# The last gate block's working tiles moved into idle buffers, its two halves interleaved, and three output weight loads given other tiles

## The chip, the cores and the metric

The kernel runs on one core of one Trainium2 chip. The metric is the device time of one execution in microseconds (us). Each version is run several times and the median is compared; a trace of one profiled execution shows where the time goes. All times below are from the start of that execution's span.

## The reference

One decoder block over 1024 positions and width 1024, in float32. What matters here, cut from the reference:

```python
h = rmsnorm(x, norm_g[l]) * (1.0 + scale) + shift
q, k, v, g_attn, xr, g_rnn, m_attn, m_rnn = split(h @ w_in[l])
y_attn = sliding_window_attention_with_sinks(q, k, v, sinks) * silu(g_attn)
xr = causal_depthwise_conv(xr, conv_w, conv_b)               # width 4
# RG-LRU: per block of 256 channels
r = sigmoid(xr @ wa + ba);  i = sigmoid(xr @ wx + bx)
a = exp(-LRU_C * r * softplus(-lam));  b = sqrt(1 - a*a) * (i * xr)
hs[t] = a[t] * hs[t-1] + b[t]                                # scan over time
y_rnn = hs * silu(g_rnn)
merged = sigmoid(m_attn) * (y_attn @ w_attn_proj) + sigmoid(m_rnn) * (y_rnn @ w_rnn_proj)
x = x + gate * (merged @ w_out);  return rmsnorm(x, final_g)
```

## The kernel before

**Products in three terms.** Every float32 operand of TensorE is split into a high part (a cast by ScalarE, `wh`, `nh`, `hh`, `mh`) and the remainder (a subtraction by VectorE, `wl`, `nl`, `hl`, `ml`); a product is high·high + low·high + high·low. `cast` (L101) makes `wh`, `rest` (L107) makes `wl`; both have five buffers.

**The projection stage.** Pairs of column blocks of `w_in` go through a seven-product scheme (`Pair`, L533 forms the weight sums `ws`, L571 joins two results). One product is 12 matmuls of 128x512 (L511) and fills one *slot*; a pair takes seven slots, k = 0 to 6, whose moving operands are named hha, nh, nh, nh, hh, hh, nh in this order. In slot 1 TensorE needs the low part of S1, in slot 5 that of S4, in slot 6 that of S3, in slot 0 that of A11: always from the second matmul of the slot on, for which VectorE must have run L107. Loads of raw weights are `r<-w_main`. L614 is the tanh of a result `c`, and `smr_d<-c` stores it.

**The recurrent branch** runs inside this stage in four blocks `hb`, each of two halves `oc`, so eight chunks c = 2·hb + oc of 128 channels. The convolution leaves `xch` (tag `xa`, two buffers) and `xcl` (tag `xcl`, two buffers). `extra` puts the gate product (24 matmuls, L794, tile `pgate`) of a half between two slots. `after_gates` then lists the ten pieces that follow for a half:

- ScalarE: Sigmoid to `rz` (a1, L809) and to `it` (a2, L812), Tanh to `th` (a3, L824), Exp to `av` and Square (a4, a5, L827, L830), Sqrt (a6, L837), the cast `yh` (a7, L852).
- VectorE: `rz` scaled (d1, L815), `it`·conv (d2, L819), `th` (d3, L833), `it` (d4, L840), the scan (d5, L845), `rz`·`gg` (d6, L849), the remainder `yl` (d7, L856).

`gg` is the silu gate, read back from DRAM (`sgr_d`); its tile shares a buffer with `th` (tag `th`, one buffer), and its load is issued at the end of d4. `yl` shares the buffer `it`, and `yh` the buffer `av`. `start_gates` queues these pieces, with gaps of a slot; `background` puts a piece on its engine when its planned time fits. Each engine then works its own list in this fixed order.

**Opening of attention.** After the last piece of c = 7 the pool of the recurrent branch (tags rz, it, th, av, xc, xcl, xa) is closed and the attention pool is opened over it: `sink`, `ks`, `qs` are loaded by SP, and the first score product (`s_ps`, L1033) follows in TensorE's list. One pair of the projection stage and the RNN projection (`rp`) are interleaved with attention.

**The tail.** `merged` is made per chunk (`tt`, L1487 to L1501). `load_wo(k)` loads a chunk of `w_out` into `wo32` (tag `tt`, two buffers, shared with the merge), multiplies it by the gate row (L1454), casts it (L1457) and subtracts (L1458); the last product (L1522) runs over eight row tiles, the first three of them together, by chunk k. Here a list scheduler sets the order. `tail` is a pool with the tags `xo` (x reloaded), `o` (three buffers for results) and `fst`.

SP issues nearly all DMAs, one queue in order; it waits for the release of a buffer before it issues the load into it, and what is behind waits too.

Of the kernel before, what the change touches and what calls it, by code (L numbers as in the profile page):

```python
# [12 lines left out]
F32 = mybir.dt.float32  # L13
# [9 lines left out]
P = 128  # L23
S = 1024
D = 1024
KC = 8
# [25 lines left out]
def tile_hybrid_block(ctx, tc, x, pk, rows, posr, posi, invf, c_row, w_ss, w_gate, w_main, w_v,  # L52
# [4 lines left out]
    def dma(dst, src, eng=nc.sync):  # L57
        dst, src = (a.bitcast(F32) if a.dtype == F32R else a for a in (dst, src))
        return eng.dma_start(dst, src)  # L59
# [75 lines left out]
    sgr_d = [tc.dram_tile([P, S], F32, name=f"sgr_d{c}") for c in range(KC)]  # L135
# [5 lines left out]
    hb = ctx.enter_context(tc.tile_pool(name="hb", bufs=1))  # L141
# [37 lines left out]
    with ExitStack() as st:  # L179
# [102 lines left out]
        tt = tiny("tt")  # L282
# [114 lines left out]
    W = {}  # L397
# [69 lines left out]
    waiting = [], []  # L467
# [15 lines left out]
    def slots(d):  # L483

        t = []

        def f():
            t.append(W["slot"])
            return W["slot"] >= t[0] + d
        return f  # L490
# [258 lines left out]
    def ask(hb, oc):  # L749

        if ("g", (hb, oc)) not in W and (hb, oc) not in gq:
            gq.append((hb, oc))
        return ("g", (hb, oc)) in W

    def second(hb):

        gq.append((hb, 1))
        W["free", hb, 1] = Load.act + 0.4
        return True

    def start_gates(hb):

        load1, split1 = gate_weights(hb, 1)
        c0, c1 = after_gates(hb, 0), after_gates(hb, 1)
        waiting[0].append(lambda: ask(hb, 0))
        one, two = [], [lambda: ask(hb, 1)]
        for todo, steps_ in ((one, c0), (two, c1)):
            for i, step in enumerate(steps_):
                gap = hb < 3 or i in ((0, 3, 5) if todo is one else (0, 3, 5, 7))
                todo.extend(step + ([slots(1)] if gap else []))  # L770
                if todo is one and i == 1:
                    todo.append(lambda: second(hb))
        if hb == 3:
            one.insert(0, lambda: W.setdefault("rush", True))
        waiting[0].extend(one + two)
        waiting[1].extend([load1, slots(2)] + split1)
        return True

    def extra():

        if not gq or Load.pe < max(W.get((n_, *gq[0]), d_) for n_, d_ in (
                ("ready", 1e9), ("free", 0.0))):
            return 0.0
        hb, oc = gq.pop(0)
        wh, wl = W["gw", hb, oc]
        res = []
        for which in range(2):
            ps = psm.tile([P, 1024], F32, tag="main", name="pgate")
            for ic in range(2):
                h_, l_ = W["xc", hb, ic][:2]  # L790
                c0 = which * 256 + ic * P
                for i, (ww, xx_) in enumerate(((wh, h_), (wl, h_), (wh, l_))):
                    for hf in range(2):
                        W["pe"] = T.matmul(ps[:, SL[hf]], ww[:, c0:c0 + P], xx_[:, SL[hf]],  # L794
                                           start=(ic == 0 and i == 0),
                                           stop=(ic == 1 and i == 2))
            res.append(ps)
        W["g", (hb, oc)] = res
        return GATE

    def after_gates(hb, oc):
        c, t = 2 * hb + oc, {}

        def tl(n, tag=None, dt=F32):
            t[n] = W["rn"].tile([P, S], dt, tag=tag or n, name=n)
            return t[n][:]

        def a1():
            A.activation(tl("rz"), W["g", (hb, oc)][0][:], AF.Sigmoid, bias=pcol(PK_BA, c))  # L809

        def a2():
            A.activation(tl("it"), W["g", (hb, oc)][1][:], AF.Sigmoid, bias=pcol(PK_BX, c))  # L812

        def d1():
            V.scalar_tensor_tensor(out=t["rz"][:], in0=t["rz"][:], scalar=pcol(PK_BSH, c),  # L815
                                   in1=rbig[:], op0=ALU.mult, op1=ALU.max)

        def d2():
            V.tensor_tensor(out=t["it"][:], in0=t["it"][:], in1=W["xc", hb, oc][2][:],  # L819
                            op=ALU.mult)  # L820
            W["used", c] = True

        def a3():
            A.activation(tl("th"), t["rz"][:], AF.Tanh)  # L824

        def a4():
            A.activation(tl("av"), t["rz"][:], AF.Exp, scale=-1.0)  # L827

        def a5():
            A.activation(t["rz"][:], t["av"][:], AF.Square)  # L830

        def d3():
            V.scalar_tensor_tensor(out=t["th"][:], in0=t["rz"][:], scalar=1.0, in1=t["th"][:],  # L833
                                   op0=ALU.add, op1=ALU.mult)

        def a6():
            A.activation(t["th"][:], t["th"][:], AF.Sqrt, scale=2.0 ** 20)  # L837

        def d4():
            V.scalar_tensor_tensor(out=t["it"][:], in0=t["th"][:], scalar=2.0 ** -10,  # L840
                                   in1=t["it"][:], op0=ALU.mult, op1=ALU.mult)
            dma(tl("gg", "th"), sgr_d[c])

        def d5():
            V.tensor_tensor_scan(out=t["rz"][:], data0=t["av"][:], data1=t["it"][:],  # L845
                                 initial=0.0, op0=ALU.mult, op1=ALU.add)

        def d6():
            V.tensor_tensor(out=t["rz"][:], in0=t["rz"][:], in1=t["gg"][:], op=ALU.mult)  # L849

        def a7():
            A.copy(tl("yh", "av", F32R), t["rz"][:])  # L852
            dma(yh_d[c], t["yh"][:], G if c == KC - 1 else nc.sync)

        def d7():
            V.tensor_tensor(out=tl("yl", "it", F32R), in0=t["rz"][:], in1=f32(t["yh"][:]),  # L856
                            op=ALU.subtract)
            dma(yl_d[c], t["yl"][:], G if c == KC - 1 else nc.sync)

        return [[[("A", 2.4, 0, a1)]], [[("A", 1.11, 0, a2), ("D", 0, 1.28, d1)]],  # L860
                [[("A", 2.35, 0, a3)], [("D", 0, 1.22, d2)]],
                [[("A", 1.06, 0, a4), ("A", 1.06, 0, a5)]], [[("D", 0, 1.22, d3)]],
                [[("A", 2.35, 0, a6)]], [[("D", 0, 1.22, d4)], [("D", 0, 2.29, d5)]],
                [[("D", 0, 1.22, d6)]], [[("A", 1.05, 0, a7)]], [[("D", 0, 1.22, d7)]]]

# [506 lines left out]
    late, high, loaded = [], [], {}  # L1372
# [76 lines left out]
    wo = [None] * KC  # L1449

    def load_wo(k, pool, tag):
        w32 = tpool.tile([P, D], F32, tag="tt", name="wo32", bufs=2)
        dma(w32[:], w_out[k * P:(k + 1) * P, :])
        V.tensor_tensor(out=w32[:], in0=w32[:], in1=gate_bc[:], op=ALU.mult)  # L1454
        t = pool.tile([P, 2, D], F32R, tag=tag, name="wo")
        h_, l_ = t[:, 0, :], t[:, 1, :]
        A.copy(h_, w32[:])  # L1457
        V.tensor_tensor(out=l_, in0=w32[:], in1=f32(h_), op=ALU.subtract)  # L1458
        wo[k] = (h_, l_)
# [197 lines left out]
```

## Time and profile before

| what | value |
|---|---|
| median of 3 runs | 937.59 us (937.12 to 939.36) |
| the profiled execution, its own time | 937.05 us |
| its span, first to last instruction | 935.3 us |
| TensorE matmuls busy | 908.0 us of the span (97%) |
| VectorE busy | 688.0 us (74%) |
| ScalarE busy | 533.7 us (57%) |
| GpSimd busy | 109.0 us (12%) |
| mean granted TensorE clock | 0.996 |

In the profile's rows the first number is the start, the second the duration, both in us; "x12" is a count of instructions merged into a row; brackets at the end give the idle time of the engine before the row and what ended it. PE is TensorE, ACT is ScalarE, DVE is VectorE, POOL is GpSimd, SPq is the DMA queue of SP. In a table of windows the columns behind the stretch are its length, the busy time of each engine with the number of its instructions, the granted clock of TensorE, the busy share of the DMA engines, and GB/s.

### The profile page before, as it was taken

Reading aid. Unit: us, or ns where it says so; the run is one execution under the profiler, and the core shown is the slowest. Engines: PE = TensorE matmul, PEld = TensorE weight load, DVE = VectorE, ACT = ScalarE, POOL = GpSimd, SP = SyncE. Lnnn points to the kernel's source line nnn. Section 1 sums busy time; section 2 is a strip of 40 time slices with the busy share of each in tenths; the row PEclk is TensorE's granted clock in tenths of the full one; section 3 lists DMA queues with packets and bytes.
Section 4 is the critical chain, followed back from the end, with each engine's and each line's share of the span. In section 5 each row is a group of like instructions: output and inputs, shape, how many; then the busy total and the mean of one; then the engine's idle time right before and its main releaser. Section 6 shows DMA issues by size and latency. Waiting matters only on the chain.

```text
span 935.3 us, 12434 instructions
## 1 busy us (share of the span) xinstructions
PE 908.0 (97%) x4261; PEld 752.4 (80%) x4261; DVE 688.0 (74%) x1068; ACT 533.7 (57%) x1040; POOL 109.0 (12%) x161
## 2 busy tenths in 40 slices
PE   5899999999999999999999988999999999999997
PEld 3689888878888888888887877888888888888786
DVE  8978888777669965996676675899999737656522
ACT  7435565454567656775696584888888622212311
POOL 1046000000000000000000001354454300000000
PEclk9999999999999999999999999999999999999999
DMA  8923587951332541354145348997655186436311
GB/s 313 374 68 125 167 283 231 310 191 46 113 112 91 187 151 50 136 175 136 57 157 170 101 138 280 320 333 238 218 177 188 57 315 224 159 125 234 132 72 67
DMA packets 81141, 164.20 MB, mean 176 GB/s; under 512 B 12772, under 2 KB 29156, under 8 KB 81079
## 3 DMA queue, kind: packets, MB, share of 16 engines
q1 hardware_dynamic: 77734, 155.32, 49.0%
q0 software_dynamic: 2192, 6.00, 1.9%
q10 hardware_dynamic: 1152, 2.10, 0.6%
q8 instruction: 33, 0.54, 0.2%
q14 instruction: 30, 0.24, 0.1%
HBM read 114.00 MB, written 49.78 MB: 175 GB/s over the span
## 4 chain that ended last, share of the span: by engine, by line
PE 75%; DVE 10%; DMA 6%; ACT 5%; issue 4%; SPq 0%; POOL 0%; ACTq 0%; DVEq 0%
PE bk L511 41%; PE rp L169 9%; PE pmain L169 4%; PE pgate L794 4%; PE rp L1522 3%; PE pmain L1522 3%; PE s_ps L1033 3%; PE pv L1105 2%; DMA wo<-w_out 2%; DMA tt<-tr_d 1%; PE pt L1071 1%; DVE wl L107 1%; PE bk L169 1%; DMA smr<-smr_d 1%; DVE wo L1458 1%
## 5 line engine op out<-in xcount | busy, mean ns | idle before, releaser
L511 PE MATMUL bk<-nh,wl 128*128 128x512 f32 x368 | 144.4, 392 | 3.7 <-DVE wl L107 3.7
L511 PE MATMUL bk<-nl,wh 128*128 128x512 f32 x368 | 143.9, 391 | 0.0
L511 PE MATMUL bk<-nh,wh 128*128 128x512 f32 x368 | 143.9, 391 | 0.0
L107 DVE TENSOR_TENSOR wl<-r,wh 128x512 fp32r<-128x512 f32 x108 | 79.0, 735 | 18.3 <-ACT wh L101 18.3
L511 PEld LDWEIGHTS bk<-nh,wl 128*128 128x128 f32 x368 | 69.4, 189 | 19.9 <-DVE wl L107 5.5
L101 ACT CAST wh<-r 128x512 fp32r<-128x512 f32 x108 | 66.4, 618 | 32.4 <-DMA r<-w_ap 12.3
L511 PEld LDWEIGHTS bk<-nh,wh 128*128 128x128 f32 x368 | 69.5, 189 | 14.4
L511 PEld LDWEIGHTS bk<-nl,wh 128*128 128x128 f32 x368 | 69.5, 189 | 14.3
L511 PE MATMUL bk<-hh,wl 128*128 128x512 f32 x184 | 71.8, 390 | 1.7 <-DVE wl L107 1.7
L511 PE MATMUL bk<-hh,wh 128*128 128x512 f32 x184 | 71.6, 389 | 0.0
L511 PE MATMUL bk<-hl,wh 128*128 128x512 f32 x184 | 71.6, 389 | 0.0
L59 POOL DMA_DIRECT2D yh_d<-yh x1 | 0.6, 583 | 479.2 <-ACT yh L852 479.2
L107 DVE TENSOR_TENSOR wl<-ws,wh 128x512 fp32r<-128x512 f32 x80 | 54.2, 681 | 1.9 <-ACT wh L101 1.9
L1057 ACT ACTIVATE p<-p,small 128x129 f32<-128x129 f32 x128 | 50.1, 400 | 0.0
L101 ACT CAST wh<-ws 128x512 fp32r<-128x512 f32 x80 | 48.0, 615 | 2.2 <-DVE ws L533 1.2
L511 PEld LDWEIGHTS bk<-hh,wl 128*128 128x128 f32 x184 | 34.6, 188 | 9.6 <-DVE wl L107 2.6
L511 PEld LDWEIGHTS bk<-hh,wh 128*128 128x128 f32 x184 | 34.6, 188 | 7.2
L511 PEld LDWEIGHTS bk<-hl,wh 128*128 128x128 f32 x184 | 34.5, 188 | 7.1
L1033 PE MATMUL s_ps<-ks,qs 128*128 128x256 f32 (+1 forms) x256 | 37.6, 289 | 0.1
L1539 ACT ACTIVATE o<-xo 128x1024 f32<-128x1024 f32 (+2 forms) x10 | 8.9, 889 | 47.5 <-DVE xo L1538 47.5
L511 PE MATMUL bk<-hha,wh 128*128 128x512 f32 x92 | 35.9, 391 | 0.0
L511 PE MATMUL bk<-hha,wl 128*128 128x512 f32 x92 | 35.8, 389 | 0.0
(356 smaller groups left out, 2255.6 us busy)
## 6 DMA issues: line engine op xcount, KB each, us to landing
r<-w_main SPq DMA_DIRECT2D x100, 256.0 KB, 4.1
wada<-w_ss SPq DMA_DIRECT2D x16, 512.0 KB, 8.4
qs<-q_d SPq DMA_DIRECT2D x16, 512.0 KB, 5.4
ks<-k_d SPq DMA_DIRECT2D x24, 192.0 KB, 3.8
xt<-x SPq DMA_DIRECT2D x8, 512.0 KB, 6.3
q_d<-rhi SPq DMA_DIRECT2D x16, 256.0 KB, 3.9
q_d<-rlo SPq DMA_DIRECT2D x16, 256.0 KB, 2.9
wg<-w_gate SPq DMA_DIRECT2D x8, 512.0 KB, 4.6
```

Source lines behind the costliest of these rows:

```text
L101: A.copy(dst[0][:], src)
L107: V.tensor_tensor(out=dst[1][:], in0=src, in1=f32(dst[0][:]), op=ALU.subtract)
L169: mm = T.matmul(ps[hf], ww, xx[kc][hf], start=(kc == 0 and ww is w_h and xx is xh), stop=(kc == KC - 1 and xx is xl))
L511: W["pe"] = T.matmul(ps, ww[:, c], b[kc][xx_], start=(first and kc == 0 and i == 0), stop=(kc == 3 and i == 2), skip_group_check=not first)
L794: W["pe"] = T.matmul(ps[:, SL[hf]], ww[:, c0:c0 + P], xx_[:, SL[hf]], start=(ic == 0 and i == 0), stop=(ic == 1 and i == 2))
L1033: W["pe"] = T.matmul(o, qs[:, j, qc], ks[:, b, k0 + (0 if n else P):k0 + 256], start=(b == 0), stop=(b == 1))
L1057: A.activation(px[:, j, :], px[:, j, :], AF.Exp, bias=sm[:, 0, j:j + 1], accum_out=sm[:, 1, j:j + 1])
L1071: W["pe"] = T.transpose(pt[:, j, :], px[:, j, 0:P], ident[:])
L1105: W["pe"] = T.matmul(pv[:], b, m[:].rearrange("p j q -> p (j q)"), start=(i == 0), stop=(i == len(prods) - 1))
L1458: V.tensor_tensor(out=l_, in0=w32[:], in1=f32(h_), op=ALU.subtract)
L1522: T.matmul(ps[:, sl], lhs[k][th][:, ts_], w[:, sl], start=(k == 0 and w is h_ and lhs is mh), stop=(k == KC - 1 and lhs is ml))
L1539: A.activation(o[:, sl], xo[:, sl], AF.Square, accum_out=fs[:, i:i + 1])
```

## The change

Four edits, three of them for the last block (hb = 3, c = 6 and 7):

1. The `gg` of c = 6 and c = 7 get tiles of the tag `xcl` (dead once the gate product of c = 7 has read it) and are both loaded directly behind that product, instead of at the end of their d4.
2. `rz` and `it` of c = 7 get tiles of the tag `xa` (dead at the same time) in place of the buffers of c = 6.
3. `start_gates` lists the pieces of the two halves interleaved: the Sigmoid a1 of c = 7 goes before the last pieces of c = 6.
4. The `wo32` of k = 4, 5 and 6 use the tag `o` of the pool `tail` in place of `tt`.

```diff
@@ start_gates
-        one, two = [], [lambda: ask(hb, 1)]
-        for todo, steps_ in ((one, c0), (two, c1)):
...
+        if hb < 3:
...
+        else:
+            gap = [None]
+            for item in ([[lambda: W.setdefault("rush", True)], c0[0], gap, c0[1],
+                          [lambda: second(hb)], c0[2], c0[3], gap, c0[4], c0[5], gap, c0[6],
+                          [lambda: ask(hb, 1)], c1[0], c0[7], gap, c0[8], c1[1], c0[9], c1[2],
+                          c1[3], gap, c1[4], c1[5], gap, c1[6], c1[7], gap, c1[8], c1[9]]):
+                waiting[0].extend([slots(1)] if item is gap else item)
@@ extra
         W["g", (hb, oc)] = res
+        if (hb, oc) == (3, 1):
+            for c in (KC - 2, KC - 1):
+                W["gg", c] = W["rn"].tile([P, S], F32, tag="xcl", name="gg", bufs=2)
+                dma(W["gg", c][:], sgr_d[c])
@@ after_gates
         def tl(n, tag=None, dt=F32):
-            t[n] = W["rn"].tile([P, S], dt, tag=tag or n, name=n)
+            late = c == KC - 1 and n in ("rz", "it")
+            t[n] = W["rn"].tile([P, S], dt, tag="xa" if late else tag or n, name=n,
+                                bufs=2 if late else 1)
@@ d4
-            dma(tl("gg", "th"), sgr_d[c])
+            if hb < 3:
+                dma(tl("gg", "th"), sgr_d[c])
+            else:
+                t["gg"] = W["gg", c]
@@ load_wo
-        w32 = tpool.tile([P, D], F32, tag="tt", name="wo32", bufs=2)
+        w32 = (tail.tile([P, D], F32, tag="o", name="wo32", bufs=3) if 4 <= k < 7 else
+               tpool.tile([P, D], F32, tag="tt", name="wo32", bufs=2))
```

No instruction is added or removed except rows that merge differently; the lists differ at the places below and, in the tail, in TensorE's order. In the changed kernel's text the lines of these pieces are higher by 11 to 15 (L849 becomes L863, L856 becomes L870, L815 becomes L826).

**VectorE, from the scan of c = 6.** Before: the product with `gg` stands directly behind the scan, ahead of both `wl` (the first is the low part of S4, the second of S3).

```order
L845 SCALAR_TENSOR_TENSOR rz<-av,it 128x1024
L849 TENSOR_TENSOR rz<-rz,gg 128x1024
L107 TENSOR_TENSOR wl<-ws,wh 128x512
L856 TENSOR_TENSOR yl<-rz,yh 128x1024
L107 TENSOR_TENSOR wl<-ws,wh 128x512
L533 TENSOR_TENSOR ws<-r 128x512
L571 TENSOR_TENSOR c<-u_4935,bk_71 128x512
L107 TENSOR_TENSOR wl<-r,wh 128x512
L533 TENSOR_TENSOR ws<-ws,r 128x512
L815 SCALAR_TENSOR_TENSOR rz<-rz,pk_t,rbig 128x1024
L819 TENSOR_TENSOR it<-it,xc 128x1024
L571 TENSOR_TENSOR c<-bk_69,p_4862 128x512
```

Now:

```order
L859 SCALAR_TENSOR_TENSOR rz<-av,it 128x1024
L107 TENSOR_TENSOR wl<-ws,wh 128x512
L863 TENSOR_TENSOR rz<-rz,gg 128x1024
L107 TENSOR_TENSOR wl<-ws,wh 128x512
L533 TENSOR_TENSOR ws<-r 128x512
L826 SCALAR_TENSOR_TENSOR rz<-rz,pk_t,rbig 128x1024
L870 TENSOR_TENSOR yl<-rz,yh 128x1024
L571 TENSOR_TENSOR c<-u_4938,bk_71 128x512
L107 TENSOR_TENSOR wl<-r,wh 128x512
L533 TENSOR_TENSOR ws<-ws,r 128x512
L830 TENSOR_TENSOR it<-it,xc 128x1024
L571 TENSOR_TENSOR c<-bk_69,p_4862 128x512
```

The low part of S4 now precedes the product with `gg`, and d1 of c = 7 precedes `yl` of c = 6 and three rows of weight work.

**ScalarE, from the Sqrt of c = 6.** Before (L809 and L812 are the Sigmoids of c = 7, L852 the cast of c = 6):

```order
L837 ACTIVATE th<-th 128x1024
L614 ACT_TABLE_LOAD
L614 ACTIVATE c<-bk_70 128x512
L101 CAST wh<-ws 128x512 x2
L560 COPY u_4935<-bk_69 128x512
L852 CAST yh<-rz 128x1024
L809 ACT_TABLE_LOAD
L809 ACTIVATE rz<-pgate,pk_t 128x1024
L614 ACTIVATE c<-bk_68 128x512
L101 CAST wh<-r 128x512
L101 CAST wh<-ws 128x512
L812 ACTIVATE it<-pgate,pk_t 128x1024
```

Now:

```order
L848 ACTIVATE th<-th 128x1024
L614 ACT_TABLE_LOAD
L614 ACTIVATE c<-bk_70 128x512
L101 CAST wh<-ws 128x512
L820 ACT_TABLE_LOAD
L820 ACTIVATE rz<-pgate,pk_t 128x1024
L101 CAST wh<-ws 128x512
L560 COPY u_4938<-bk_69 128x512
L614 ACTIVATE c<-bk_68 128x512
L101 CAST wh<-r 128x512
L866 CAST yh<-rz 128x1024
L823 ACTIVATE it<-pgate,pk_t 128x1024
```

The first Sigmoid of c = 7, with its table load, now precedes the cast `yh` of c = 6 and the second cast of weights; the second Sigmoid directly follows the cast.

**SP's queue at the same place** (`sgr_d_139` is the gate of c = 6, `sgr_d_140` of c = 7):

```order
 L59 DMA r<-w_main 128x512 x3
+L59 DMA gg<-sgr_d_139 128x1024
+L59 DMA gg<-sgr_d_140 128x1024
 L59 DMA smr_d_110<-c 128x512
 L59 DMA r<-w_main 128x512
-L59 DMA gg<-sgr_d_139 128x1024
+L59 DMA smr_d_111<-c 128x512
 L59 DMA yh_d_123<-yh 128x1024
 L59 DMA yl_d_131<-yl 128x1024
```

Both loads of `gg` now stand ahead of a store of `c` and one weight load; the second stood some ten DMAs further on, ahead of the last store before `sink`.

**VectorE in the tail** (`wo32_8151` is chunk k = 3, 8157, 8163, 8169 are k = 4, 5, 6, 8175 is k = 7; L1454 and L1469 are the multiplication by the gate row, L1458 and L1473 the remainder). Before:

```order
L1501 TENSOR_TENSOR ml_8130<-tt_8122,mh_8129 128x512 x2
L1454 TENSOR_TENSOR wo32_8151<-wo32_8151,gate_bc_7553 128x1024
L1458 TENSOR_TENSOR wo_8154<-wo32_8151,wo_8154 128x1024
L1454 TENSOR_TENSOR wo32_8157<-wo32_8157,gate_bc_7553 128x1024
L1454 TENSOR_TENSOR wo32_8163<-wo32_8163,gate_bc_7553 128x1024
L1458 TENSOR_TENSOR wo_8160<-wo32_8157,wo_8160 128x1024
L1458 TENSOR_TENSOR wo_8166<-wo32_8163,wo_8166 128x1024
L1454 TENSOR_TENSOR wo32_8169<-wo32_8169,gate_bc_7553 128x1024
```

Now:

```order
L1469 TENSOR_TENSOR wo32_8157<-wo32_8157,gate_bc_7553 128x1024
L1516 TENSOR_TENSOR ml_8130<-tt_8122,mh_8129 128x512 x2
L1469 TENSOR_TENSOR wo32_8163<-wo32_8163,gate_bc_7553 128x1024
L1469 TENSOR_TENSOR wo32_8151<-wo32_8151,gate_bc_7553 128x1024
L1469 TENSOR_TENSOR wo32_8169<-wo32_8169,gate_bc_7553 128x1024
L1473 TENSOR_TENSOR wo_8154<-wo32_8151,wo_8154 128x1024
L1473 TENSOR_TENSOR wo_8160<-wo32_8157,wo_8160 128x1024
L1473 TENSOR_TENSOR wo_8166<-wo32_8163,wo_8166 128x1024
```

The multiplications of k = 4 and 5 now precede that of k = 3, and four multiplications precede the first remainder. In SP's queue the loads of k = 4 and 5 now follow `fg_bc` directly, then k = 3 and 6, and the four loads of `xo` come behind these.

More of the change, by code (lines that the diff above doesn't have):

```diff
@@ L765, in start_gates @@
         waiting[0].append(lambda: ask(hb, 0))
-        one, two = [], [lambda: ask(hb, 1)]
-        for todo, steps_ in ((one, c0), (two, c1)):
[L768 to L775, printed above, removed]
+        if hb < 3:
+            one, two = [], [lambda: ask(hb, 1)]
+            for todo, steps_ in ((one, c0), (two, c1)):
+                for i, step in enumerate(steps_):
+                    todo.extend(step + [slots(1)])
+                    if todo is one and i == 1:
+                        todo.append(lambda: second(hb))
+            waiting[0].extend(one + two)
+        else:
[5 more added lines that the diff above has]
+                waiting[0].extend([slots(1)] if item is gap else item)
         waiting[1].extend([load1, slots(2)] + split1)
```

## Prediction

> **What bounds the kernel.** I read the page first, then the windows of the stage that the change touches, its list of waits, and the timelines of each engine there.
>
> ```profile
> PE 908.0 (97%) x4261; PEld 752.4 (80%) x4261; DVE 688.0 (74%) x1068; ACT 533.7 (57%) x1040; POOL 109.0 (12%) x161
> 99.31 92.48 PE bk L511 x408
> ```
>
> The second row is from the chain that ended last. TensorE is the bound, so what can be won is its idle and its slow time. An undisturbed stretch gives its pace: 92.48 / 408 = 0.2267 us per matmul, 2.72 us per product of 12. The windows, the first counting L511 alone, show where it loses that pace:
>
> ```profile
> 532.00:575.20 43.20, 38.15 (x156) 29.92 (x155) 0.96 0.59 195
> 839.90:871.00 31.10, 30.32 (x132) 24.44 (x132) 18.09 (x16) 7.45 (x8) 0.00 (x0) 1.00 0.55 186
> 575.20:600.00 24.80, 24.80 (x139) 21.47 (x138) 18.56 (x33) 18.86 (x63) 6.28 (x13) 1.00 0.93 304
> ```
>
> From the end of the last gate product to the first scores there are 156 matmuls, 13 products: 35.4 us at pace, 43.20 taken, so 7.8 us lost, 5.05 of it idle. In the tail 132 matmuls make 29.9 us of 31.10: 1.2 us lost. Right behind the first stretch TensorE has no idle time, though the DMA engines are 0.93 busy. TensorE's own rows name the places:
>
> ```profile
> 538.67 0.50 PE L511 MATMUL bk<-hh,wl 128*128 128x512 f32 x1 [0.85 <-DVE wl L107]
> 547.81 0.50 PE L511 MATMUL bk<-nh,wl 128*128 128x512 f32 x1 [0.68 <-DVE wl L107]
> 559.89 0.50 PE L511 MATMUL bk<-hh,wl 128*128 128x512 f32 x1 [0.90 <-DVE wl L107]
> 565.53 0.68 PE L511 MATMUL bk<-nh,wl 128*128 128x512 f32 x1 [2.63 <-DVE wl L107]
> 566.01 0.63 PE L511 MATMUL bk<-nl,wh 128*128 128x512 f32 x1
> ...
> 569.28 0.39 PE L511 MATMUL bk<-nh,wl 128*128 128x512 f32 x1
> 575.20 1.00 PE L1033 MATMUL s_ps<-ks,qs 128*128 128x128 f32 x8
> ```
>
> Four low parts come late: of S4, S1, S4 and S3. After the longest wait nine steps (565.53 to 569.28) take 3.75 us instead of 2.04: the granted clock, 0.96 in that stretch, has fallen, and that costs 1.7 us more. Why VectorE is late:
>
> ```profile
> 530.63 2.29 DVE L845 TENSOR_TENSOR_SCAN rz<-av,it 128x1024 f32<-128x1024 f32 x1
> 536.79 1.22 DVE L849 TENSOR_TENSOR rz<-rz,gg 128x1024 f32<-128x1024 f32 x1 [3.87 <-DMA gg<-sgr_d]
> 537.94 0.68 DVE L107 TENSOR_TENSOR wl<-ws,wh 128x512 fp32r<-128x512 f32 x1
> ...
> 543.82 1.28 DVE L815 SCALAR_TENSOR_TENSOR rz<-rz,pk_t,rbig 128x1024 f32<-128x1024 f32 x1
> 545.34 1.22 DVE L819 TENSOR_TENSOR it<-it,xc 128x1024 f32<-128x1024 f32 x1 [0.24 <-ACT it L812]
> ...
> 547.08 0.68 DVE L107 TENSOR_TENSOR wl<-ws,wh 128x512 fp32r<-128x512 f32 x1
> ...
> 555.70 1.23 DVE L840 SCALAR_TENSOR_TENSOR it<-th,it 128x1024 f32<-128x1024 f32 x1 [1.89 <-ACT th L837]
> 556.96 2.29 DVE L845 TENSOR_TENSOR_SCAN rz<-av,it 128x1024 f32<-128x1024 f32 x1
> 559.17 0.66 DVE L107 TENSOR_TENSOR wl<-ws,wh 128x512 fp32r<-128x512 f32 x1
> 563.65 1.22 DVE L849 TENSOR_TENSOR rz<-rz,gg 128x1024 f32<-128x1024 f32 x1 [3.82 <-DMA gg<-sgr_d]
> ```
>
> Twice VectorE, which works in order, stands 3.8 us before the product with `gg` while a weight remainder is queued behind it. The S1 and the second S4 are late because c = 7's chain is late as a whole; its start is on ScalarE:
>
> ```profile
> 538.10 1.05 ACT L852 CAST yh<-rz 128x1024 fp32r<-128x1024 f32 x1 [2.60 <-DVE rz L849]
> 539.17 1.28 ACT L809 ACT_TABLE_LOAD   x1
> 540.46 1.12 ACT L809 ACTIVATE rz<-pgate,pk_t 128x1024 f32<-128x1024 f32 x1
> 544.18 1.12 ACT L812 ACTIVATE it<-pgate,pk_t 128x1024 f32<-128x1024 f32 x1 [1.09 <-DMA yl_d<-yl]
> 545.20 1.05 ACT L824 ACTIVATE th<-rz 128x1024 f32<-128x1024 f32 x1
> 554.61 1.06 ACT L837 ACTIVATE th<-th 128x1024 f32<-128x1024 f32 x1
> ```
>
> **The loads of `gg`.** The new tiles wait for the last reads of `xcl`:
>
> ```profile
> 530.18 0.62 PE L794 MATMUL pgate<-xcl,wh 128*128 128x512 f32 x2
> 531.54 0.62 PE L794 MATMUL pgate<-xcl,wh 128*128 128x512 f32 x2
> 532.17 0.41 SPq L59 DMA_DIRECT2D gg<-sgr_d  x1
> 558.50 0.41 SPq L59 DMA_DIRECT2D gg<-sgr_d  x1
> ```
>
> So the load for c = 6 can leave at 530.8 instead of 532.17, and with the 4.6 us from its issue to the product above it lands near 535.4; I take 536.0, since the second, issued at 532.2 instead of 558.50, shares its way. The second lands near 538 and is needed past 555: its wait of 3.8 us goes. SP stands until 532.2 with a store of `c` and one weight load (A12) behind; both leave about 2 us later. That weight is first needed two slots into the next pair, past 548; its cover is ten us. The store frees one of five `c` buffers, with a pair's time to spare. Both cost nothing.
>
> **VectorE and ScalarE, slot by slot**, in times of the old clock, products at 532.00 + 2.72·n if none waits. The first S4 remainder now follows the scan directly: 532.9 to 533.6; TensorE wants it in n = 2 at 537.7. Wait 1 (1.0 us with its restart) goes, with 4 us to spare. Product with `gg` 536.1 to 537.3, S3's remainder to 537.9 (wanted 540.4), `ws`, d1 of c = 7 at 538.5 to 539.7 instead of 543.82. ScalarE has the first Sigmoid long done (about 534: its inputs, half of the gate product, are there before 530). With its table load it takes 2.4 us and pushes one weight cast back by as much; VectorE wants that only at 537.3. ScalarE then does the cast `yh` (to 539.8), the second Sigmoid without the 1.09 us for the store of `yl`, since `it` has another buffer, a weight cast, and the Tanh at 541.3 instead of 545.20: 3.9 us earlier. `yl` of c = 6 waits for `yh` until 539.9 and holds the next remainder (A11) to 542.2, wanted 543.1. d2, the join and S1's remainder end at 545.2, wanted at 545.8: wait 2 goes with 0.6 to spare. From Tanh to Sqrt 9.4 us as before: Sqrt at 550.8 to 551.9. d4 and scan to 555.4, the second S4 remainder to 556.0, wanted at 556.7: wait 3 goes with 0.7 to spare. The product with `gg` follows without a wait to 557.1, S3's remainder to 557.8, wanted 559.4: wait 4 goes, and with it what starts the clock's fall. Sum: up to 7.8 us. Two margins are 0.6 and 0.7, so I leave 0.3 and take 7.5.
>
> [...]
>
> **Opening of attention.** `sink` now waits for the product with `gg` of c = 7 (it lies over `xcl`), at 557.1 by the above, not for a gate product long past. Ahead of it in SP's queue is the store of a `c` whose tanh needs the result of n = 8, about 557.5.
>
> ```profile
> 560.11 0.33 SPq L59 DMA_DIRECT2D sink<-rows  x1
> 562.32 0.55 SPq L59 DMA_DIRECT2D qs<-q_d  x1
> DMA to landing us min/median/max: 3.9/5.4/8.8
> ```
>
> The last row is for `qs`. `sink` leaves at 558.0, `qs` 2.2 later, landing at 565.6 with the median. Scores come at 532.0 + 35.4 = 567.4. Cost nothing with 1.8 us to spare; with the maximum 1.6 us late.
>
> **The tail.**
>
> ```profile
> 851.23 1.22 DVE L1454 TENSOR_TENSOR wo<-wo,gate_bc 128x1024 f32<-128x1024 f32 x1
> 863.84 1.22 DVE L1454 TENSOR_TENSOR wo<-wo,gate_bc 128x1024 f32<-128x1024 f32 x1 [2.08 <-DMA wo<-w_out]
> 867.60 2.48 DVE L1458 TENSOR_TENSOR wo<-wo,wo 128x1024 fp32r<-128x1024 f32 x2
> 854.24 0.62 PE L1522 MATMUL rp<-wo,hh 128*128 128x512 f32 x2
> 868.87 0.74 PE L1522 MATMUL rp<-wo,mh 128*128 128x512 f32 x2 [0.70 <-DVE wo L1458]
> ```
>
> With two buffers each multiplication of a late chunk waits for its load (2.1 us for k = 6), and TensorE for the remainder of k = 6, ready at 868.8. Now k = 4, 5, 6 load ahead. But the multiplications of k = 4 and 5 stand before that of k = 3. The first falls partly into the time in which VectorE waits for a cast, the second costs its 1.2 us: k = 3 is multiplied at about 853.0 instead of 851.23, and its high part is there 2.4 us later (851.23 to 853.62 before, when the remainder could start), at 855.4. TensorE, with two matmuls of another tile moved ahead (854.24 + 0.45), wants it at 854.7 and waits 0.7. From there the remainders follow each other by 1.2: k = 3 at 856.6 (wanted 856.8), k = 6 at 860.3, k = 7 at 863.9, none wanted before. So 1.2 lost becomes 0.8: I take 0.4 won. The ends: 1.2 won if k = 3 is in time; 1.6 lost if its load lands 2 us later, since it waits in SP's queue as before but the others now share the engines. The four loads of `xo` move behind two chunks, still some 15 us ahead of the first sum; they cost nothing.
>
> **Sum.** 937.05 - 7.5 - 0.4 = 929.2 for the profiled execution; the median of the runs lies 0.5 above it (937.59), so 929.7. Measurements of this kernel tell about 0.3%, 2.8 us, from no change.
>
> **Rivals.**
>
> *The pair of `gg` loads crowd each other.* If the first lands with the second, as late as 539.2 (532.2 + 4.6 + half of a load), S3's remainder ends at 541.1 (0.7 late), d1 at 542.9, the Tanh starts 1.7 later and the second S4 is 1.0 late: 931.4. For it: both are issued within 1.4 us. Against: in this stretch the DMA engines are only 0.59 busy. [...]
>
> *The attention operands become the last to land.* Their lead on the scores shrinks from 12.9 us (562.32 to 575.20) to 7.2, and c = 7's two stores of 512 KB leave in the same time. With the maximum of 8.8 us TensorE waits 1.6, with some clock lost 3: 931 to 933. The median speaks against it.
>
> *The gain is given back behind the opening.* There the DMA engines are 0.93 busy for 25 us; if the transfers and not TensorE set that stretch, half of 7.5 is lost: 933.5. TensorE's unbroken 24.80 of 24.80 us speaks against it.
>
> *The clock falls all the same.* Then 1.7 us of the sum stay lost: 931.4. Against it: the slow rows begin right behind the longest wait and nowhere else in that stretch. [...]
>
> *The change does not do what it says*, c = 7 stays late and only the two waits for `gg` go: 1.0 + 2.8 + 1.7 less what the scan then costs; 3 won, 934.5, or less.
>
> *Slower.* The wait of `sink` on c = 7's product with `gg` holds the opening. From that product's end to the landing of `qs` are 0.9 + 2.2 + 5.4 = 8.5 us. The scores then come at its end + 8.5, and the time passes 940.4 (2.8 above before) only if they come after 578.0 + 0.4, that is, if the product ends past 569.9: 12.8 us later than worked out, 5 us later than before (564.9). Something would have to hold c = 7's chain for a whole extra round; no row shows it.
>
> **How the numbers follow.** Forecast as summed, 928.5 to 931: 0.60. Crowded loads 0.08, the clock 0.02, late operands 0.12, given back behind the opening 0.08 (all still faster), the change without its effect 0.06 (half of it faster), slower 0.03, and 0.01 for no effect at all. Faster by over 0.3%: 0.60 + 0.30 + 0.03 = 0.93, which I lower to 0.89 for mechanisms not thought of; same 0.07, slower 0.04. The range: from 928.2 (all 7.8 and 1.2 won, 937.05 - 9.0 = 928.1) up to 933.8, which takes in the first four rivals.
>
> **What would show it.** Right: no wait of VectorE for `gg` beyond 1 us for c = 6 and none for c = 7; the Tanh of c = 7 some 9.5 us after the gate product; 13 products in 36 us or less from the gate product to the scores; a clock of 1.00 there; TensorE waiting in the tail for the high part of k = 3 and not for k = 6. Wrong: an idle time of TensorE before the first scores, waits for `wl` of S1 or S4 in the second pair, or new idle time between 575 and 610.

## The result, and the profile after

| | before | after |
|---|---|---|
| median of 6 runs each, side by side | 937.53 us (935.56 to 939.36) | 932.59 us (930.62 to 934.70) |
| ratio | | 0.9947, 95% interval 0.9929 to 0.9965 |
| profiled execution, its own time | 937.05 us | 934.70 us, the longest of the six |
| its span | 935.3 us | 933.0 us |

The change makes the kernel 0.53% faster. 929.7 was forecast: of 7.9 us, 4.9 came. The windows of the changed kernel (columns as before, clock ahead of the last two) say where:

```profile
532.00:568.00 36.00, 35.44 (x157) 29.02 (x155) 26.62 (x33) 26.01 (x36) 2.39 (x5) 1.00 0.58 206
568.00:575.20 7.20, 5.30 (x17) 4.56 (x18) 1.89 (x3) 1.59 (x3) 0.90 (x3) 0.62 1.01 302
575.20:600.00 24.80, 24.80 (x137) 21.23 (x136) 17.89 (x32) 17.86 (x60) 6.37 (x12) 0.97 0.85 275
835.00:871.00 36.00, 36.00 (x161) 29.77 (x160) 23.61 (x24) 10.93 (x14) 0.00 (x0) 1.00 0.44 161
```

In the first row 157 matmuls stand where before had 128 in the same 36 us: the four waits for `wl` are gone, and the 0.56 us of idle time is the beginning of another wait. In the second row that wait goes on, and the clock is 0.62. The tail is busy throughout. VectorE's and ScalarE's rows for the chain of c = 6 and 7:

```profile
534.10 1.23 DVE L863 TENSOR_TENSOR rz<-rz,gg 128x1024 f32<-128x1024 f32 x1 [0.66 <-DMA gg<-sgr_d]
536.44 1.28 DVE L826 SCALAR_TENSOR_TENSOR rz<-rz,pk_t,rbig 128x1024 f32<-128x1024 f32 x1
541.03 1.07 ACT L835 ACTIVATE th<-rz 128x1024 f32<-128x1024 f32 x1
550.46 1.06 ACT L848 ACTIVATE th<-th 128x1024 f32<-128x1024 f32 x1
552.81 2.29 DVE L859 TENSOR_TENSOR_SCAN rz<-av,it 128x1024 f32<-128x1024 f32 x1
555.02 0.67 DVE L107 TENSOR_TENSOR wl<-ws,wh 128x512 fp32r<-128x512 f32 x1
555.60 1.22 DVE L863 TENSOR_TENSOR rz<-rz,gg 128x1024 f32<-128x1024 f32 x1
558.69 1.23 DVE L870 TENSOR_TENSOR yl<-rz,yh 128x1024 fp32r<-128x1024 f32 x1 [0.67 <-ACT yh L866]
```

The waits of 3.87 and 3.82 us for `gg` are 0.66 and none, and the remainder of S4 (555.02) now stands ahead of the product. SP's rows at the opening of attention, a row from its list of waits, and TensorE's rows:

```profile
557.23 0.33 SPq L59 DMA_DIRECT2D smr_d<-c  x1
559.94 0.33 SPq L59 DMA_DIRECT2D sink<-rows  x1
561.81 0.61 SPq L59 DMA_DIRECT2D qs<-q_d  x1
```

```profile
SPq L59 <- DVE yl L870: 2.2, 1, 2.2
```

```profile
569.90 1.94 PE L1047 MATMUL s_ps<-ks,qs 128*128 128x128 f32 x8 [2.45 <-DMA qs<-q_d]
571.63 0.73 PE L511 MATMUL bk<-nh,wh 128*128 128x512 f32 x1
572.17 0.63 PE L511 MATMUL bk<-nh,wl 128*128 128x512 f32 x1
...
576.01 0.63 PE L511 MATMUL bk<-nh,wl 128*128 128x512 f32 x1
576.73 1.11 PE L1047 MATMUL s_ps<-ks,qs 128*128 128x256 f32 x8
```

`sink` leaves at 559.94, the moment at which `yl` of c = 7 ends (558.69 + 1.23 = 559.92); `qs` stands behind it and lands nearly 8 us after its issue. TensorE waits 2.45 us, then runs at half clock until the second scores: the granted clock is 0.50 from 569.90 to 576.40, and a matmul of 128x512 takes 0.63 us there, 0.39 before the wait.

To compare profiles, this table gives the lead on the profile of before at five marks and at the end: start there less start here, less the same difference at a gate product ahead of the change (507.31 before). For the changed kernel at the first scores: 575.20 - 569.90 - (507.31 - 507.23) = 5.2. The marks are the first scores (575.20), the second (578.87), the ninth (612.35), the first matmul of the attention projection (761.08), the first with the output weight (839.96) and the span's end (935.3). The kernels e1 to e12 are told of below. They were measured in three fours, each beside its own runs of before, whose medians were 937.24, 938.12 and 936.51 us: between fours the ratios compare, not the times.

| profile | 1st scores | 2nd | 9th | 761 | 840 | end |
|---|---|---|---|---|---|---|
| changed kernel | 5.2 | 2.1 | 1.2 | 0.9 | 0.9 | 2.2 |
| the same again (e12) | 5.7 | 5.6 | 5.6 | 5.4 | 5.4 | 6.7 |
| e1, `ks` and `qs` ahead of `sink` | 7.8 | 7.8 | 3.5 | 3.2 | 3.2 | 4.6 |
| e4, first edit alone | 6.2 | 6.2 | 2.0 | 2.1 | 2.1 | 2.3 |
| e5, e1 with stores by GpSimd | 7.8 | 7.8 | 7.3 | 7.6 | 7.6 | 9.0 |
| e6, e1 with stores by SP | 7.8 | 7.8 | 8.5 | 6.6 | 6.6 | 7.1 |
| e7, e1 without reloads | 7.8 | 7.8 | 7.8 | 7.9 | 7.9 | 9.2 |
| e9, stores by GpSimd alone | 7.1 | 7.0 | 6.7 | 7.1 | 7.1 | 8.5 |
| e10, e5 without edits 2, 3 | 6.2 | 6.2 | 6.6 | 6.8 | 6.8 | 8.3 |
| e11, e5 without edit 4 | 7.8 | 7.8 | 8.2 | 8.5 | 8.5 | 9.9 |

### The profile page after: what moved, and what is told of

It is laid out like the page before. It is cut to its first block, busy times and chain, and to the rows that moved or that the text cites. A ratio compares the mean times of both kernels' runs of the same rounds, so it can differ in the third digit from the quotient of the medians.

```text
span 933.0 us, 12428 instructions
## 1 busy us (share of the span) xinstructions
PE 907.5 (97%) x4261; PEld 752.7 (81%) x4261; DVE 687.9 (74%) x1068; ACT 533.5 (57%) x1040; POOL 108.4 (12%) x161
## 4 chain that ended last, share of the span: by engine, by line
PE 87%; DVE 5%; DMA 2%; ACT 2%; issue 1%; SPq 1%; POOL 0%; ACTq 0%; DVEq 0%
PE bk L511 44%; PE rp L169 12%; PE pmain L169 8%; PE rp L1537 5%; PE pgate L799 5%; PE pmain L1537 4%; PE s_ps L1047 3%; PE pv L1119 2%; PE pt L1085 1%; PE bk L169 1%; DMA qs<-q_d 1%; DMA r<-w_rp 1%; SPq L59 1%; DVE wl L107 1%; ACT xT L326 1%
## 5 line engine op out<-in xcount | busy, mean ns | idle before, releaser
L614 ACT ACTIVATE c<-bk 128x512 f32<-128x512 f32 x31 | 18.5, 598 | 32.7 <-PE bk L511 32.7
L1047 PEld LDWEIGHTS s_ps<-ks,qs 128*128 128x128 f32 x256 | 33.2, 194 | 3.8 <-issue 2.8
```

What stands on the lines that cost most here:

```text
L614: A.activation(t["t"], s(), AF.Tanh, scale=0.5)
L1047: W["pe"] = T.matmul(o, qs[:, j, qc], ks[:, b, k0 + (0 if n else P):k0 + 256], start=(b == 0), stop=(b == 1))
```

## The experiments

### First four: the opening, its control, and two edits alone

Theory A: the rest is lost at the opening of attention. In the built program `sink` lies at the place of the buffer that the second edit gives to `rz` of c = 7, which `yl` reads last (SP's wait for `yl` above agrees); `ks` and `qs` of the first scores lie elsewhere, but stand behind it in SP's queue. e1 issues them first and leaves all tiles where they are:

```diff
-        dma(W["sink"][:], rows[0:1, 2048:2048 + NH].to_broadcast([P, NH]))
-        sink(0)
+        sink(0, False)          # allocates p and small only
         load_kq(0)
+        dma(W["sink"][:], rows[0:1, 2048:2048 + NH].to_broadcast([P, NH]))
+        sink(0)
         load_kq(1)
```

> The changed kernel, with the loads of ks and qs for the first scores issued ahead of sink; the tiles keep their places, so sink still waits for the remainder yl of c = 7. Theory A (what was won ahead of the scores is lost at the opening: sink waits for yl, ks and qs stand behind it in SP's queue, qs lands 2.45 us late, and the wait brings the half clock): ks leaves at about 557.6, right behind the store of c at 557.23, qs at about 559.2, landing between 564.6 (5.4 us) and 567.2 (8 us); the first scores come at 567.3 instead of 569.9, the second at 571.0 instead of 576.7; no wait of TensorE for qs above 0.3 us, clock 1.00 there; median 929.3 (3.3 below the changed kernel), ratio to before 0.991. Rival B (the transfers set the stretch behind the opening): scores at 567.3 too, but new waits of TensorE between 575 and 610 take it back; median 931.9 to 932.6. Rival C (the stores of yh and yl fill the engines, and qs needs 8 us or more wherever it is issued): the wait only shrinks to 0.5 to 1; median 930.6 to 931.2.

Measured: 932.06 us (931.16 to 934.35, 6 runs), ratio 0.9946 (0.9933 to 0.9959), where the changed kernel had 0.9947. At the opening everything came as theory A says (SP, then TensorE): `qs` leaves 2.4 us earlier, no wait, no half clock (granted 1.00 from 560 to 580), scores at 567.50.

```profile
557.94 1.28 SPq L59 DMA_DIRECT2D ks<-k_d  x2
559.38 0.55 SPq L59 DMA_DIRECT2D qs<-q_d  x1
567.50 1.00 PE L1052 MATMUL s_ps<-ks,qs 128*128 128x128 f32 x8
```

But the lead of 7.8 us is 3.5 at the ninth scores. Rows of ScalarE, VectorE and TensorE in e1, in order of time:

```profile
574.37 0.58 ACT L614 ACTIVATE c<-bk 128x512 f32<-128x512 f32 x1
578.33 0.33 ACTq L59 DMA_DIRECT2D smr_d<-c  x1
578.70 0.62 ACT L101 CAST wh<-ws 128x512 fp32r<-128x512 f32 x1 [3.75 <-DMA hla<-yl_d]
579.83 0.73 DVE L1066 COPY_PREDICATED p<-mgt,s_ps 128x512 f32<-128x512 uint32 x1 [3.94 <-ACT p L1060]
580.62 1.21 PE L1052 MATMUL s_ps<-ks,qs 128*128 128x256 f32 x8 [1.44 <-DVE p L1066]
587.67 0.33 ACTq L59 DMA_DIRECT2D smr_d<-c  x1
588.09 0.37 ACT L1133 COPY ob<-pv 64x256 f32<-64x256 f32 x1 [2.22 <-DMA r<-w_rp]
589.83 0.47 PE L1124 MATMUL pv<-phc,vs 128*128 128x512 f32 x1 [0.46 <-ACT phc L1095]
```

ScalarE itself issues the stores of the projection's tanh results in this stage. At 574.95 the next is due, and it is issued at 578.33; the stand of 3.75 us ahead of the next cast ended with the landing of an earlier load (`hla`, issued at 571.55). The softmax behind it in ScalarE's order waits, VectorE for that (3.94 us), and TensorE for VectorE (1.44). At both stands of e1 the load has the same place in the order in which SP and ScalarE, taken together, issue their transfers: behind that `hla` come `hha`, `hla`, two `ks`, `qs`, `hha`, `hla`, and then the store, the eighth. At the second stand the store (587.67) is likewise the eighth behind the load of `r` issued at 580.71. Why it is the eighth no trace shows.

Of the 4.3 us lost up to the ninth scores, idle time of TensorE in those rows and two shorter waits behind them makes 2.4 (1.44, 0.46, 0.20, 0.28); the rest is not followed. So theory A is right on the opening and wrong on the time: rival B's sign, with a mechanism that none of the three named.

e2, the control: the same reordering in the kernel before.

> The kernel before, with the same reordering of sink and the first ks and qs. Control for e1: there the scores are set by the convolution at 575.2, with qs long landed, so theories A, B and C all expect 937.5, within 0.5, and no change at the first scores. If it falls by 1 us or more, the reordering has an effect of its own, and e1 does not tell A apart.

Measured: 937.20 us (11 runs), 0.9998 (0.9989 to 1.0006): no effect.

e3: before, with `load_wo` as in the change and nothing else.

> The kernel before with the last edit alone (k = 4, 5, 6 of the output weight loaded through the output tiles). By the trace of the changed kernel the tail (from 839 to the end) became 1.3 us shorter there, since no wait of TensorE is left in it: 936.2 (ratio 0.9986). By the prediction, where k = 3 is 0.7 to 0.8 late: 937.1 (0.9996).

Measured: 936.90 us (11 runs), 0.9994 (0.9984 to 1.0005), which doesn't tell 0 from 1.3 us. The profiles tell more. From the first matmul with the output weight to the end it is 95.3 us before (935.3 - 839.96) and 94.0 in e3 (934.2 - 840.19), as in the changed kernel (933.0 - 838.96). But of the profiles without this edit only before, e4 (95.2) and e8 (95.3) show the longer tail; e2 (94.2) and e11 (93.9) don't. The wait that the edit removes is there in some executions and not in others. Nor is the tail short in every profile with the edit: in e6 below it is 94.9.

e4: before, with the first edit alone (the lines of `extra` and d4 of the diff).

> The kernel before with the first edit alone: both gg loads of the last block issued right behind its second gate product into xcl; the halves one after the other as before, rz and it in their own buffers, the tail as before. The product with gg of c = 6 can come at about 534.1 instead of 536.79, 2.7 us earlier, and c = 7 loses its wait of 3.8. Theory A (the wait for gg was the cause of all four waits for wl, and without the second edit sink does not wait for yl): the chain of c = 7 moves 2.7 earlier, waits of 1.0, 0.7, 0.9 and 2.6 us go, sink leaves early as before, clock 1.00 in 532 to 600, scores at 567.5 to 568.5; median 930.3 (7.2 below before), below the changed kernel although it has one edit of four. Rival D (the overlap of the halves is needed): the waits for wl of S4 and S1 stay, each 0.5 to 1; median 932.5 to 935.

Measured: 934.53 us (932.89 to 936.24, 9 runs), 0.9969 (0.9960 to 0.9979). One wait for `wl` is left, and the first scores lead by 6.2 us; then ScalarE stands as in e1:

```profile
558.25 0.50 PE L511 MATMUL bk<-hh,wl 128*128 128x512 f32 x1 [1.14 <-DVE wl L107]
579.13 0.33 ACTq L59 DMA_DIRECT2D smr_d<-c  x1
579.50 0.62 ACT L101 CAST wh<-ws 128x512 fp32r<-128x512 f32 x1 [3.01 <-DMA hla<-yl_d]
589.51 0.37 ACT L1121 COPY ob<-pv 64x256 f32<-64x256 f32 x1 [2.84 <-DMA r<-w_rp]
```

The time falls into rival D's range, but not by D's waits: three of the four are gone with the `gg` loads alone.

### Second four: ScalarE freed

Theory E: ScalarE's stand at its stores eats the lead. e5 is e1 with the stores issued by GpSimd; e6 has them in SP's queue; e7 leaves out the reload of y for c = 0 and 1; e8 is before with e5's edit.

```diff
-                        dma(dst[j][:, SL[th]], t["t"], A if "att" in W else nc.sync)
+                        dma(dst[j][:, SL[th]], t["t"], G if "att" in W else nc.sync)
```

> The kernel of e1 (ks and qs ahead of sink) with the tanh stores that ScalarE issues during attention issued by GpSimd instead. In e1 the first scores came 7.7 us earlier than before, and 4.2 of that were lost again by 603: ScalarE stood 3.75 us at the issue of a store (574.9 to 578.3) until a load of yl_d had landed, and 2.2 us more at the next until a load of r had, and the softmax behind it made TensorE wait 1.44 and 0.66. Theory E (the gain is lost because ScalarE stands at the issue of its stores, each of which waits for an earlier transfer to land while the DMA engines are 0.99 busy): no idle time of ScalarE that ends with a DMA above 0.5 us between 568 and 603, no wait of TensorE for p or phc, 3 us more won: median 929.2, ratio to before 0.9915. Rival B (the transfers themselves set the stretch): the waits move to loads (qs, hha or r), and the median stays at 931.5 to 932.5.

Measured: 928.17 us (927.54 to 928.99, 4 runs), 0.9898 (0.9879 to 0.9917). A window of e5, and its only row of TensorE there with a wait:

```profile
568.00:600.00 32.00, 30.73 (x170) 26.23 (x170) 24.23 (x44) 24.39 (x78) 11.77 (x24) 1.00 1.00 342
```

```profile
594.33 0.47 PE L1124 MATMUL pv<-phc,vs 128*128 128x512 f32 x1 [1.27 <-DMA vs<-vs_d]
```

The DMA engines are 1.00 busy, the stand is gone, and TensorE loses only 1.27 us in these 32, to a load. So the crowd of transfers by itself does not set this stretch; in e1 it did through ScalarE, which stood 3.75 and 2.22 us. The edit does a second thing: in e1 SP stands 7.1 us, until a store of ScalarE has landed, before the `qs` that it issues at 569.11, and in e5 that `qs` leaves at 562.57. e7 below keeps this stand of SP and is as fast as e5, so ScalarE's stand is the one that counts.

> As e5, but the stores go through SP's queue, put off to the next point at which stores are flushed. Theory E expects ScalarE as free as in e5; SP now stands for the tanh and for the earlier transfers instead, with the loads of the next ks and qs behind it: median 929.5, up to 930.5 if those come late. Rival B: 931.5 to 932.5, as e1.

The edit puts `store(dst[j][:, SL[th]], t["t"])` in that line. Measured: 929.34 us (928.98 to 929.93, 4 runs), 0.9911 (0.9892 to 0.9929), as theory E expects: no idle time of TensorE in 568 to 600. Later it waits once, 1.2 us, for a load of `yl`.

```diff
-            for i in range(2):
-                dma(hs[i], yh_d[c][:, SL[i]])
-                dma(ls[i], yl_d[c][:, SL[i]])
```

> The kernel of e1 without the eight loads of hha and hla right behind the opening (c = 0 and 1 of y, 2 MB; the products then use what lies in these tiles). It tells whether the crowd of transfers behind the opening makes the landings late. Theories E and B both expect the engines below 0.85 busy between 568 and 600, qs landing in 5 us or less, ScalarE's stand below 1 us, and a median of 929.2. If the late landings have another cause (the order of the queues, or the stores of yh and yl ahead), ScalarE's stand stays and the median with it, at 931.5 to 932.

Measured: 928.00 us (927.71 to 928.57, 5 runs), 0.9896 (0.9878 to 0.9914). With less in flight (DMA engines 0.85 busy, 1.00 in e5) the store is issued at 575.40 with no stand:

```profile
568.00:600.00 32.00, 32.00 (x182) 27.73 (x181) 24.89 (x46) 24.59 (x79) 9.66 (x19) 1.00 0.85 276
```

```profile
575.40 0.36 ACTq L59 DMA_DIRECT2D smr_d<-c  x1
```

The median landing of `qs` says nothing here: it is 4.6 us over all sixteen, and was 4.5 in e1. With the reloads ScalarE's stand goes, as theories E and B expect. Two things change at once, though: fewer transfers are in flight, and with these loads gone another transfer stands eighth ahead of the store. The run does not tell these apart.

> The kernel before with the tanh stores of attention issued by GpSimd. Control for e5: before, ScalarE stood only 1.3 us at such an issue (596.1), and TensorE waited for nothing in 575 to 600, so theory E and rival B both expect 937.2, down to 936.7. If it falls by 2 us or more, the gain of e5 is one of its own and not that of the change given back.

Measured: 937.05 us (12 runs), 0.9990 (0.9979 to 1.0001), against 938.12. (The 1.3 us at 596.1 are no such stand: no transfer ends them in the rows of before, where ScalarE's stores leave at 582.68 and 591.03 without one.) What e5 wins is not a gain of that edit alone; the edit keeps what the change wins.

### Last four: the corners, and the changed kernel again

e9 is the changed kernel with e5's line and without e1's edit.

> The changed kernel with the tanh stores of attention issued by GpSimd, but sink still ahead of ks and qs (e5 without e1's edit). With it the four corners are there: changed kernel 932.59, e1 932.06 (ks and qs first), e5 928.17 (both). Theory E with the late qs as a second cause of its own: qs still lands 1 to 2.5 us late and brings some half clock, so the median lies at 930 to 931.5, 2 to 3.5 above e5. If the stand of ScalarE is the only cause and the wait for qs costs nothing that is not lost behind it anyway, the median is that of e5, 928.2 to 928.8. If both are needed together, it stays at 932 to 932.6.

Measured: 929.34 us (928.55 to 930.71, 5 runs), 0.9923 (0.9910 to 0.9936), below the expected range in time, where e5 has 928.17. By the ratios it is 2.3 us above e5, as a late `qs` as a cause of its own would have it, and the two intervals overlap, so the times do not decide. The profiles differ by 0.5 us in their lead at the end (8.5 and 9.0). The opening in e9:

```profile
561.89 0.55 SPq L59 DMA_DIRECT2D qs<-q_d  x1
568.13 1.08 PE L1047 MATMUL s_ps<-ks,qs 128*128 128x128 f32 x8 [0.62 <-DMA qs<-q_d]
```

`qs` leaves as late as in the changed kernel but the wait is 0.62 us, not 2.45. The two stores that ScalarE issued at 561.21 and 563.43 there leave GpSimd at 565.39 in e9. So in this profile the one line serves both places, `qs` and the stand; that it is the stores that slowed `qs` fits the order of these times, but was not tried alone.

e10 is e5 with `after_gates`'s buffers and `start_gates` as before (edits 2 and 3 undone); e11 is e5 with `load_wo` as before (edit 4 undone).

> e5 without the second and third edit of the change: of the last block only the gg loads are early; the halves stand one after the other, rz and it have their own buffers; the tail's edit, ks and qs ahead of sink and the stores by GpSimd stay. In e4 the first scores came 6.2 us earlier than before, against 7.7 in e1, with one wait of 1.1 us for wl. Expected: 1.3 to 1.5 above e5, 929.6. If the overlap of the halves does more than that wait shows: 930.5 or more; if it is worth nothing: 928.2.

Measured: 929.76 us (928.62 to 930.42, 5 runs), 0.9922 (0.9910 to 0.9934): as expected in time, and 2.2 us above e5 by the ratios, whose intervals overlap. By the profiles the buffers and the overlap are worth 7.8 - 6.2 = 1.6 us at the first scores, the early `gg` loads the rest.

> e5 without the last edit (the output weight's chunks through two buffers, as before). e3 left it open whether that edit wins 0 or 1 us (0.9994, 0.9984 to 1.0005). By the traces (1.2 us of wait gone, no new one) 929.3; by the prediction's 0.4 won, 928.6.

Measured: 927.83 us (927.02 to 930.20, 4 runs), 0.9907 (0.9891 to 0.9922). In time that is 0.3 us below e5, by the ratios 0.8 above; it can't be told from no effect. What the last edit is worth on the average of runs stays open between 0 and 1.3 us.

> The changed kernel once more, unchanged, on the same chip and with a second profile. Its median stands at 932.6 (930.6 to 934.7 over six runs). If the wait for qs varies from run to run, as theory E needs for that spread, this profile shows a wait other than 2.45 us (0 to 2.5), less half clock, and in its place the stand of ScalarE behind the opening, with nearly the same time at the end: 931 to 933.5. If the late qs alone were the cause, a shorter wait would show in a shorter time one for one and no stand of ScalarE.

Measured: 931.14 us (930.19 to 933.47, 6 runs), 0.9943 (0.9928 to 0.9957); the profiled execution took 930.29. TensorE's rows and a window:

```profile
569.53 1.08 PE L1047 MATMUL s_ps<-ks,qs 128*128 128x128 f32 x8 [2.01 <-DMA qs<-q_d]
573.27 1.11 PE L1047 MATMUL s_ps<-ks,qs 128*128 128x256 f32 x8
```

```profile
568.00:575.20 7.20, 5.67 (x33) 5.01 (x34) 2.05 (x4) 2.37 (x5) 0.90 (x3) 1.00 1.00 312
```

The wait for `qs` is there again, 2.01 us, but no half clock behind it, and against theory E no stand of ScalarE either: its store comes due 2 us later than in e1 and is issued at 577.07 with no load to wait for. From first to second scores it is 3.74 us here and 6.83 in the first profile: the half clock cost 3.1 us there. The mean clocks of the runs go the same way: of the twelve runs of the changed kernel the four with 0.998 or 0.999 took 930.2 to 930.6, the eight with 0.996 or 0.997 took 931.6 to 934.7. But a mean clock does not say where it fell. The profiled execution of e5 has 0.996 too, with no slow stretch at the opening and one at 15 to 30 us, where before has 1.00:

```profile
15.00:30.00 15.00, 11.92 (x59) 10.09 (x58) 14.19 (x33) 13.52 (x31) 1.18 (x2) 0.89 1.01 383
```

So in both profiled executions of the changed kernel the largest loss is at the late `qs`, in one of them with the half clock behind it; how often that comes in the other ten runs is not shown. The stand of ScalarE is what comes next in e1, where `qs` is early.

## Why the prediction was right, and where it was not

**The number.** 932.59 us lies in the stated range, but not in the 928.5 to 931 of the forecast as summed: the range reaches so far because it takes in the rivals, and one of them happened. Idle time of TensorE before the first scores, which the prediction named as a sign of being wrong, is there.

**The four waits: right.** Up to 7.8 us was worked out, 7.5 taken. Wherever `qs` is not waited for (e1, e5, e6, e7, e11) the lead at the first scores is 7.8.

| step | forecast | changed kernel |
|---|---|---|
| product with `gg`, c = 6 | 536.1 | 534.10 |
| d1 of c = 7 | 538.5 | 536.44 |
| Tanh | 541.3 | 541.03 |
| Sqrt | 550.8 | 550.46 |
| second S4 remainder starts | 555.4 | 555.02 |
| product with `gg`, c = 7 | 556.0 | 555.60 |
| `sink` issued | 558.0 | 559.94 |
| `qs` issued | 560.2 | 561.81 |
| first scores | 567.4 | 569.90 |

**The opening: the step that failed.** "`sink` now waits for the product with `gg` of c = 7 (it lies over `xcl`)" named the wrong buffer. It lies over the `xa` buffer that the second edit had just given to `rz`, so it waits for the last reader of that, `yl`, which ends at 559.92, not for the product that was put at 557.1; it left 1.9 us later than worked out. And `qs` was taken at its median of 5.4 us, though four stores leave in its way: it took nearly 8. Together the two use up the 1.8 us to spare and give the 2.45 us of wait. The stores, GpSimd's of c = 7 and ScalarE's, in the changed kernel:

```profile
558.95 0.58 POOL L59 DMA_DIRECT2D yh_d<-yh  x1 [471.87 <-ACT yh L866]
560.22 0.54 POOL L59 DMA_DIRECT2D yl_d<-yl  x1 [0.68 <-DVE yl L870]
561.21 0.37 ACTq L59 DMA_DIRECT2D smr_d<-c  x1
563.43 0.33 ACTq L59 DMA_DIRECT2D smr_d<-c  x1
```
The rival that names this (attention operands last to land, 931 to 933) got 0.12; it is what happened, and the median lies in its 931 to 933. It had 1.6 us of wait and 3 lost with some clock; in the profiled run the late scores cost 2.6 and the half clock 3.1 more.

**The gain given back behind the opening** occurred in e1 and e4, by 4.3 and 4.2 us (7.8 - 3.5, 6.2 - 2.0), not in e12, and by at most 1.2 in the changed kernel's first profile, where ScalarE stands 1.28 us at one store (589.71). The argument against it, TensorE's unbroken 24.80 us, was read from a profile in which the loads had time to land: before, the next store was due 7.4 us after the first of these `hla` loads (575.21, 582.64), in e1 3.4 us (571.55, 574.95); the four loads of `hla` took 5.9 to 7.0 us from issue to landing before and 6.4 to 7.5 in e1.

**The tail: 0.4 forecast, 1.3 in the profiles that have the wait.** The high part of k = 3 was to be 0.7 late. In the changed kernel it was not: VectorE (first two rows) takes the first of the moved chunks at 847.32, when it would wait for a cast, and reaches k = 3 at about 851.1, not 853.0; TensorE wants it at 853.70 and does not wait.

```profile
847.32 1.23 DVE L1469 TENSOR_TENSOR wo<-wo,gate_bc 128x1024 f32<-128x1024 f32 x1
849.83 3.67 DVE L1469 TENSOR_TENSOR wo<-wo,gate_bc 128x1024 f32<-128x1024 f32 x3
853.70 0.63 PE L1537 MATMUL rp<-wo,hh 128*128 128x512 f32 x2
```

In e6, which has the edit too, the forecast wait is there, 0.56 us for that high part. VectorE takes the first of the moved chunks 9.6 us after the tail's first matmul (833.33, 842.90) there, against 8.4 us in the changed kernel (838.96, 847.32):

```profile
848.78 0.73 PE L1542 MATMUL rp<-wo,hh 128*128 128x512 f32 x2 [0.56 <-ACT wo L1477]
```

**The sum** for the profiled execution, by the leads: 7.8 - 2.6 (late scores) - 3.1 (half clock) - 1.2 (small waits behind it, not followed further) + 1.3 (tail) = 2.2, which is 935.3 - 933.0 but for 0.1. In e12's profile: 7.8 - 2.1 - 0.3 + 1.3 = 6.7. The crowded `gg` loads and the slower case did not occur: VectorE waits 0.66 us for the first `gg`, and the product for c = 7 ends at 556.8.

## What to carry to other kernels

When dead buffers are put to new use, look up in the built program what lies over them next: here the first tile of the next stage did, and SP, with everything behind it in its queue, waited 2.2 us for a late reader. In a stretch as crowded as this one (DMA engines 0.99 busy in e1 from 575.20 to 600) it is better not to have an engine that computes issue transfers: ScalarE stood there 3.75 and 2.22 us at the issue of two stores until an older load had landed, and all its work with it. A lead won ahead of a crowded stretch is safe only once the next waits (here `qs`, then ScalarE's stores) are found and moved: e1 alone won nothing over the changed kernel; with one more line (e5) it takes 928.17 us, 0.9898 of before, an interval that ends (0.9917) below where those of both measurements of the changed kernel begin (0.9928 and 0.9929).

## What the runs showed of the hardware that was not expected

Six of the fourteen profiles have a wait of TensorE of over 2 us between 532 us and the first scores, of 2.01 to 3.29 us. Behind four of these the half clock followed, behind two it did not, and their length does not part them: it followed 2.45 us in the changed kernel and not 2.66 us in e8. These rows of TensorE are the longest waits there of three kernels with the old transition, e2, e3 and e8 in this order, all for `wl`:

```profile
566.86 0.80 PE L511 MATMUL bk<-nh,wl 128*128 128x512 f32 x1 [3.29 <-DVE wl L107]
```

```profile
565.79 0.50 PE L511 MATMUL bk<-nh,wl 128*128 128x512 f32 x1 [2.76 <-DVE wl L107]
```

```profile
566.37 0.50 PE L511 MATMUL bk<-nh,wl 128*128 128x512 f32 x1 [2.66 <-DVE wl L107]
```

Matmuls of 0.63 us follow the first two, as they follow 2.63 us before and 2.45 in the changed kernel; none follow 2.66 us in e8 or 2.01 in e12. The granted clock from 560 to 580 is 0.91 before, in e2 and in e3, 0.83 in the changed kernel, 1.00 in e8 and e12. The half clock cost 1.7 us before and 3.1 us in the changed kernel.
